# Sample-group state products of a hybrid decoder step: full-size SSD blocks, queue passes between tiny products, GLA sample queries built earlier

## The chip, the core and the metric

One core of a Trainium2 chip runs the whole step. TensorE multiplies into PSUM; VectorE (DVE), ScalarE (ACT) and GpSimd (POOL) work beside it; SyncE (SP) and POOL issue DMAs. The metric is the device time in microseconds (us) of one execution. Lower is better.

## The reference, cut to what matters

Two trunk layers work on 288 token columns: 256 prompt tokens and 32 sample tokens (8 sequences of 4). Each layer projects x with many weight matrices, runs three mixers (SSD, mLSTM, GLA), gates and merges them, and then runs a PEER expert stage. Each mixer carries a state; for the sample group each of the 8 sequences has its own state, which its 4 tokens read and then update. The read of the SSD state is the second term of `y`:

```
y = (jnp.einsum('btsgh,bsghp->btghp', w, xc)
     + jnp.einsum('btgn,bghpn->btghp', cc, h) * jnp.exp(lam)[..., None])
```

There are 2 groups g of 4 heads h, with 64 state rows n and 64 channels p. In GLA the read is `qc * exp(lam)` times S, with 4 heads of 64 by 128; in mLSTM it is C times q, with 4 heads of 128 by 128.

## The kernel before, in words

**The queue of passes.** Each layer's large projections are a list of jobs (`self.jobs`). A generator `feed` (L300) works them off: for each of 8 row blocks of one 128-column weight block it issues three passes of 288 columns (L325, L327, L329: high part by high, high by low, low by high), so a column block is 24 passes. Before a half block is multiplied, ACT (L210) rounds its weights to the high part and DVE (L211) subtracts to get the low part; these splits are issued three halves ahead. `pump(n)` issues the next n passes, and returns without any when the list is empty.

**The mixers.** `ssd`, `mlstm` and `gla` are generators. `mixers` (L392) steps each that is alive once per round, and after every step pumps `RATE` passes (18 with two alive, 6 with three, 14 with two once the SSD branch is queued). The order of instructions on every engine is therefore written out by hand: this loop fixes it. All three go over two prompt chunks of 128 tokens and then the sample segment of 32.

**The list of jobs.** 63 column blocks do not wait for the end of mLSTM or GLA: 51 from the start, then the 4 of the SSD branch and 8 gates, which `ssd` adds at its end. Only when mLSTM ends does `branch(1, ...)` add 4 blocks of its branch and 4 gates (to 71). GLA's end adds 4, and then 8 of the output projection (83).

**The SSD sample segment.** `ch` (L641) is the decayed query, with group g on partitions 64g to 64g+63. For each of 8 heads two sorts of products add into `py`: `w` by `xdt` (L656), and 8 products, one per sequence, of a 64x64 state `hS` with 4 columns of `ch` (L663). Two heads form a step, then the generator yields: 4 steps. L669 adds the skip term. `START` passes are pumped before the first chunk.

**mLSTM sample states.** 8 units (head, half of the sequences): 4 products of a 128x128 state with 4 columns (L895), one update product (L898), then a yield.

**GLA sample states.** `QS` (L1096) is the query with one head's rows kept, made by two DVE instructions at the start of the sample segment. L1104 adds the local part into `pos`, then 4 units of 4 products of a 128x128 state `SS` with 8 columns of `QS` (L1117). POOL makes masked values for the updates in `masked` (its instruction is L380) of mLSTM and GLA. `QE`, from which `QS` is made, is complete at L1043, after the last decay level.

**mLSTM's end.** After the last unit come the norm, a wait until the gates are projected (`until`, then `sigmoids` L486 and the GLA gate's sigmoids L949, each pumping 4 passes), a table load for exponentials (L358), the split of the branch (L957, L960, L962) and `branch(1)`. `merge` (L1210) normalises at the layer's end.

Of the kernel before, what the change touches and what calls it, by code (L numbers as in the profile page):

```python
# [7 lines left out]
F32 = mybir.dt.float32  # L8
# [8 lines left out]
OP = mybir.AluOpType  # L17
# [5 lines left out]
TP = 256  # L23
# [13 lines left out]
STEPS = 76  # L37
SIGM = 4
SIGS = 6
START = 24  # L40
NO = 2
NG = 8
NB = 16
# [23 lines left out]
def bc(ap, shape):  # L67
    return ap.to_broadcast(shape)


class Kernel:
# [483 lines left out]
    def ssd(self):  # L555
        ve, ac, gp, pe, L, I, O, mx = self.ve, self.ac, self.gp, self.pe, self.L, self.I, self.O, self.mx
        act4, act2, dt = self.xs, self.bcs, self.dt
# [21 lines left out]
        ys = act4  # L579
        self.pump(START)  # L580
        yield 1
        for sg, (c0, n) in enumerate(SEGS):
            cols = slice(c0, c0 + n)
            smp = sg == 2
            if sg == 1:
# [6 lines left out]
                hS = [self.st2(f"hS{i}", [128, 2, 4, 64], I["h"][L][:, 2 * i:2 * i + 2]) for i in range(4)]  # L592
# [12 lines left out]
            xdt = self.w2("xdt")  # L605
# [13 lines left out]
            r4 = lambda a: a[:, :4 * n].rearrange("p (h t) -> p h t", t=n)  # L619
            w = []  # L620
            for g in range(2):
                pd = r4(self.ps_rc("pd"))
                for h4 in range(4):
                    pe.matmul(pd[:n, h4], bc(self.ident[:8, g * 4 + h4:g * 4 + h4 + 1], [8, n]), lam[:, cols],
                              start=True, stop=True)
# [11 lines left out]
            if sg:  # L637
                el = r4(self.w2("el", n))
                ac.activation(el, pl, AF.Exp)
                ch = r4(self.w2("ch", n))  # L640
                ve.tensor_tensor(ch, el, bc(act2[:, None, 1, cols], [128, 4, n]), op=OP.mult)  # L641
            yield 1
            for g in range(2):
                pcb = self.ps_rc(f"pcb{g}")[:, :n]
                pe.matmul(pcb[:n], act2[g * 64:(g + 1) * 64, 0, cols], act2[g * 64:(g + 1) * 64, 1, cols],
                          start=True, stop=True)
                ve.tensor_tensor(w[g][:n], w[g][:n], bc(pcb[:n, None, :], [n, 4, n]), op=OP.mult)
            yield 1
            py = [self.ps_rc(f"py{g}")[:, :2 * n].rearrange("p (i t) -> p i t", t=n) for g in range(2)]
            for i in range(4):  # L650
                g = i // 2
                for h2 in range(2):
                    h = 2 * i + h2
                    h4 = h - 4 * g
                    po = py[g][64 * h2:64 * h2 + 64, i % 2]
                    pe.matmul(po, xdt[:n, h * 64:(h + 1) * 64], w[g][:n, h4], start=True, stop=(sg == 0),  # L656
                              skip_group_check=True)
                    if sg == 1:
                        pe.matmul(po, hP[g * 64:(g + 1) * 64, h4], ch[g * 64:(g + 1) * 64, h4],
                                  start=False, stop=True, skip_group_check=True)  # L660
                    elif sg == 2:
                        for b in range(8):
                            pe.matmul(po[:, 4 * b:4 * b + 4], hS[b // 2][g * 64:(g + 1) * 64, b % 2, h4],  # L663
                                      ch[g * 64:(g + 1) * 64, h4, 4 * b:4 * b + 4],
                                      start=False, stop=True, skip_group_check=True)
                if smp:
                    yield 1
            for i in range(4):
                ve.scalar_tensor_tensor(ys[i][:, cols], act4[i][:, cols], self.pc("sd", i), py[i // 2][:, i % 2],  # L669
                                        op0=OP.mult, op1=OP.add)  # L670
            yield 1

            if not smp:
# [10 lines left out]
            else:  # L684
                elb = el.rearrange("p h (b t) -> p b h t", t=4)
                for u in range(4):
                    ph = self.ps_rc("ph").rearrange("p (b h d) -> p b h d", h=4, d=64)
                    for b2 in range(2):
                        b = 2 * u + b2
# [28 lines left out]
        hi, lo = self.z4("bsh", F32R), []  # L718
# [8 lines left out]
    def mlstm(self):  # L727
        ve, ac, gp, pe, L, I, O, mx = self.ve, self.ac, self.gp, self.pe, self.L, self.I, self.O, self.mx
# [7 lines left out]
        b = self.row("b", 4)  # L736
# [47 lines left out]
        for sg, (c0, n) in enumerate(SEGS):  # L784
            cols = slice(c0, c0 + n)
            smp = sg == 2
            N4 = 4 * n
            r4 = lambda a: a[:, :N4].rearrange("p (h t) -> p h t", t=n)
# [90 lines left out]
            for h in range(4):  # L879
                pe.matmul(pn[:, h], vt[:n, h * 128:(h + 1) * 128], St[:n, h], start=(h == 0 or not smp), stop=(sg == 0),  # L880
                          skip_group_check=True)
# [4 lines left out]
            if smp:  # L886
                yield 1
                for u in range(8):
                    h, bh = divmod(u, 2)
                    if u + 2 < 8:  # L890
                        load(u + 2)
                    S = CS[u]
                    for b_ in range(4):
                        t0 = 16 * bh + 4 * b_
                        pe.matmul(pn[:, h, t0:t0 + 4], S[:, b_], qe[:, h, t0:t0 + 4], start=False, stop=True,  # L895
                                  skip_group_check=True)
                    pc_ = self.ps_rc("pc_").rearrange("p (b d) -> p b d", d=128)
                    pe.matmul(pc_, kst[:96, h * 128:(h + 1) * 128], vm[:96], start=True, stop=True)  # L898
                    if u < 7:
                        vm = mask(u + 1)  # L900
                    ve.tensor_tensor(S, S, bc(ec[:, h, 2 + 4 * bh:6 + 4 * bh].unsqueeze(2), [128, 4, 128]), op=OP.mult)
                    ve.tensor_tensor(S, S, pc_, op=OP.add)
                    gp.dma_start(O["sC"][L][:, h, 4 * bh:4 * bh + 4], S)
                    yield 1
# [8 lines left out]
            if not smp:  # L913
                pc_ = hd(self.ps_rc("pc_"))
                for h in range(4):
                    pe.matmul(pc_[:, h], kt[:n, h * 128:(h + 1) * 128], wv[:n, h * 128:(h + 1) * 128],
                              start=True, stop=True)
# [36 lines left out]
        hi, lo = self.z4("bmh", F32R, "mk"), self.z4("bml", F32R, "mv")  # L954
# [12 lines left out]
    def gla(self):  # L967
        ve, ac, gp, pe, L, I, O, mx = self.ve, self.ac, self.gp, self.pe, self.L, self.I, self.O, self.mx
# [54 lines left out]
        for l in range(7):  # L1023
            X, nt = nxt
            if l < 6:
                nxt = decayed(l + 1)
            else:

                QE = s2("QE")
                ac.activation(QE, lam, AF.Exp, scale=TAU)  # L1030
                ends = mx.tile([128, 2, 10], F32, tag="ends", name="ends")
                ve.tensor_copy(ends[:, :, 0:2], lam[:, :, 127:TP:128])
                ve.tensor_copy(ends[:, :, 2:], lam[:, :, TP + 3::4])
                KE = lam
                for c0, c1, n, e in ((0, TP, 128, ends[:, :, 0:2]), (TP, T, 4, ends[:, :, 2:])):
                    a = lambda x: x[:, :, c0:c1].rearrange("p h (n t) -> p h n t", t=n)
                    ve.tensor_tensor(a(KE), bc(e.unsqueeze(3), [128, 2, (c1 - c0) // n, n]), a(lam), op=OP.subtract)
                ac.activation(KE, KE, AF.Exp, scale=TAU)
                el = mx.tile([128, 2, 8], F32, tag="el", name="el")
                ve.tensor_copy(el, QE[:, :, TP + 3::4])  # L1040
                elc = mx.tile([128, 2], F32, tag="elc", name="elc")
                ve.tensor_copy(elc, QE[:, :, TP - 1])
                ve.tensor_tensor(QE, QE, q, op=OP.mult)  # L1043
                ve.tensor_tensor(KE, KE, k, op=OP.mult)
            yield 1
            for sg, (c0, n) in enumerate(SEGS):
                if c0 < nt:
                    pa = scores(X, X, sg)
                    for h2 in range(2):
                        ve.copy_predicated(att[sg][:n, h2::2], bc(self.masks[:n, None, l, :n], [n, 2, n]), pa[h2][:n])  # L1050
# [3 lines left out]
        for sg, (c0, n) in enumerate(SEGS):  # L1054
# [35 lines left out]
                vst = self.stack("vst", pv[:32], 512, False)  # L1090
            yield 1
            if smp:

                QS = self.w2("QS", n).rearrange("p (h g t) -> p h g t", g=2, t=32)
                for h2 in range(2):
                    ve.tensor_scalar(QS[:, :, h2], QE[:, :, cols], self.half[:, h2:h2 + 1], None, op0=OP.mult)  # L1096
                pos = self.ps_rc("pos")[:, :128].rearrange("p (h g t) -> p h g t", g=2, t=32)
                po2 = [pos[:, :, h2] for h2 in range(2)]
            else:
                po2 = [self.ps_rc(f"po{h2}")[:, :2 * n].rearrange("p (h t) -> p h t", t=n) for h2 in range(2)]  # L1100
# [7 lines left out]
            if smp:  # L1108
                for u in range(4):
                    hp, bh = divmod(u, 2)  # L1110
                    if u + 2 < 4:
                        load(u + 2)
                    S = SS[u]
                    vms = [mask(2 * hp + h2, bh) for h2 in range(2)]
                    for b in range(4):
                        t0 = 16 * bh + 4 * b
                        pe.matmul(pos[:, hp, :, t0:t0 + 4], S[:, b], QS[:, hp, :, t0:t0 + 4],  # L1117
                                  start=False, stop=True, skip_group_check=True)
                    ve.tensor_tensor(S, S, bc(el[:, hp, 4 * bh:4 * bh + 4].unsqueeze(2), [128, 4, 128]), op=OP.mult)
                    yield 1  # L1120
                    pst = self.ps_rc("pst").rearrange("p (b d) -> p b d", d=128)
                    for h2 in range(2):
                        pe.matmul(pst, kz[:96, hp, h2], vms[h2][:96], start=h2 == 0, stop=h2 == 1)
                    ve.tensor_tensor(S, S, pst, op=OP.add)
                    gp.dma_start(O["sS"][L][:, hp, 4 * bh:4 * bh + 4], S)
# [682 lines left out]
```

## Time and profile before

| | |
|---|---|
| device time, median of 3 runs | 2605.63 us (2599.55 to 2611.2) |
| profiled execution, device time | 2610.51 us |
| its span in the trace | 2608.7 us |
| mean granted TensorE clock | 0.965 of full |
| TensorE busy | 2507.6 us, 96% |
| VectorE busy | 2040.0 us, 78% |
| ScalarE busy | 1283.9 us, 49% |

The mixers run from the start to about 445 us for the first layer, and from about 1290 to 1740 us for the second. A TensorE that is shown busy can still be slow: the granted clock is told beside it, as a share of 2.4 GHz, and 0.5 is the lower of its two levels (1.2 GHz).

### The profile page before, as it was taken

How to read it: one execution, taken by the hardware profiler on the slowest of the kernel's cores; microseconds unless marked ns; L12 is line 12 of the kernel's file. 1: busy time of each engine (PE TensorE's matmuls, PEld its weight loads, DVE VectorE, ACT ScalarE, POOL GpSimd, SP SyncE). 2: the span in 40 equal slices, each digit the busy share in tenths (PEclk: the TensorE clock that was granted, in tenths of full speed). 3: DMA queues.
4: the chain of work that ended last, by engine and by line, in shares of the span. 5: the costliest groups of instructions: out<-in, count | busy, mean ns of one | idle time of the engine just before them, and what ended most of it. 6: DMA issues, size and time to landing. Idle time of an engine off the chain costs nothing. (4 is left out here: it accounts for less than half of the span.)

```text
span 2608.7 us, 45575 instructions
## 1 busy us (share of the span) xinstructions
PE 2507.6 (96%) x17206; PEld 2276.1 (87%) x17206; DVE 2040.0 (78%) x4018; ACT 1283.9 (49%) x2545; POOL 359.9 (14%) x362
## 2 busy tenths in 40 slices
PE   8999998999999999999989999989999999999998
PEld 8987897989999988888789878979999999788886
DVE  7647777699899958888685477775998999588885
ACT  6433555445554434444474344653455544444444
POOL 1000232150000012221020002222400000122210
PEclk9978999999999999999999798999999999999999
DMA  5422444446555568888545124435455455689884
GB/s 167 126 72 77 147 155 130 139 145 185 163 170 160 165 196 304 302 310 299 175 134 134 58 85 163 152 110 163 158 173 171 161 170 164 227 305 305 304 276 132
DMA packets 132029, 465.11 MB, mean 178 GB/s; under 512 B 15361, under 2 KB 17537, under 8 KB 131809
## 3 DMA queue, kind: packets, MB, share of 16 engines
q1 hardware_dynamic: 109728, 385.14, 45.3%
q0 software_dynamic: 22080, 77.06, 9.3%
q8 instruction: 135, 2.21, 0.3%
q14 instruction: 86, 0.70, 0.1%
HBM read 451.32 MB, written 10.82 MB: 177 GB/s over the span
## 5 line engine op out<-in xcount | busy, mean ns | idle before, releaser
L211 DVE TENSOR_TENSOR hl<-raw,hl 128x1024 fp32r<-128x1024 f32 (+1 forms) x832 | 874.9, 1056 | 313.4 <-ACT hl L210 298.1
L210 ACT ACTIVATE hl<-raw 128x1024 fp32r<-128x1024 f32 (+1 forms) x880 | 777.4, 887 | 493.6 <-PE pu L255 153.1
L1522 PE MATMUL acc<-hl,wh 128*128 128x512 f32 x2048 | 649.2, 397 | 9.2 <-ACT hl L210 8.0
L254 PE MATMUL pu<-hh,hl 128*128 128x256 f32 x2048 | 505.1, 287 | 12.8 <-ACT WA L1442 12.8
L255 PE MATMUL pu<-hl 128*128 128x256 f32 x2048 | 495.5, 281 | 0.0
L1522 PEld LDWEIGHTS acc<-hl,wh 128*128 128x128 f32 x2048 | 386.3, 189 | 106.3 <-ACT hl L210 10.7
L1522 PE MATMUL acc<-hl,wl 128*128 128x512 f32 x1024 | 408.0, 398 | 0.0
L254 PEld LDWEIGHTS pu<-hh,hl 128*128 128x128 f32 x2048 | 388.0, 189 | 15.0 <-ACT WA L1442 14.2
L255 PEld LDWEIGHTS pu<-hl 128*128 128x128 f32 x2048 | 388.2, 190 | 0.0
L327 PE MATMUL pz<-xl,hl 128*128 128x288 f32 x1008 | 329.0, 326 | 0.6 <-DVE xl L1630 0.3
L325 PE MATMUL pz<-xh,hl 128*128 128x288 f32 x1008 | 312.5, 310 | 13.5 <-ACT xh L210 6.5
L329 PE MATMUL pz<-xh,hl 128*128 128x288 f32 x1008 | 311.2, 309 | 1.2 <-DVE hl L211 1.0
L257 PE MATMUL pu<-hh,hl 128*128 128x256 f32 x2048 | 285.9, 283 | 2.4 <-DVE hl L211 2.2
L257 PEld LDWEIGHTS pu<-hh,hl 128*128 128x128 f32 x2048 | 261.2, 189 | 3.7 <-DVE hl L211 3.4
L1522 PEld LDWEIGHTS acc<-hl,wl 128*128 128x128 f32 x1024 | 193.4, 189 | 47.8
L210 ACT ACTIVATE wh<-WA 128x256 fp32r<-128x256 f32 x200 | 83.5, 417 | 278.0 <-PE acc L1522 275.8
L325 PEld LDWEIGHTS pz<-xh,hl 128*128 128x128 f32 x1008 | 201.6, 200 | 17.0 <-ACT xh L210 7.3
L327 PEld LDWEIGHTS pz<-xl,hl 128*128 128x128 f32 x1008 | 200.9, 199 | 17.6 <-issue 12.1
L329 PEld LDWEIGHTS pz<-xh,hl 128*128 128x128 f32 x1008 | 202.1, 200 | 7.1 <-issue 3.5
L1643 POOL DMA_INDIRECT gbuf<-in_u,se x64 | 61.7, 964 | 957.3 <-PE pu L257 705.3
L1482 DVE TENSOR_TENSOR oj<-dgd,dones 128x1024 int32<-128x1024 int32 x64 | 139.2, 2178 | 0.0
L211 DVE TENSOR_TENSOR wl<-WA,wh 128x256 fp32r<-128x256 f32 x200 | 84.5, 422 | 69.3 <-ACT wh L210 69.3
(582 smaller groups left out, 3515.6 us busy)
## 6 DMA issues: line engine op xcount, KB each, us to landing
raw<-in_ut SPq DMA_DIRECT2D x256, 512.0 KB, 3.8
raw<-in_v SPq DMA_DIRECT2D x256, 512.0 KB, 4.5
raw<-in_win SPq DMA_DIRECT2D x126, 512.0 KB, 3.6
raw<-in_wq SPq DMA_DIRECT2D x32, 512.0 KB, 3.6
raw<-in_wbr SPq DMA_DIRECT2D x24, 512.0 KB, 3.6
raw<-in_wout SPq DMA_DIRECT2D x16, 512.0 KB, 3.6
CS<-in_C SPq DMA_DIRECT2D x16, 256.0 KB, 4.0
out_sC<-CS POOLq DMA_DIRECT2D x16, 256.0 KB, 3.2
```

The lines of the kernel that those rows point to most:

```text
L210: self.ac.activation(hi, r, AF.Copy)
L211: (eng or self.ve).tensor_tensor(lo, r, hi.bitcast(F32), op=OP.subtract)
L254: self.pe.matmul(ps, wh[k], self.xh[:, k, :n], start=(k == 0), stop=False)
L255: self.pe.matmul(ps, wh[k], self.xl[:, k, :n], start=False, stop=False)
L257: self.pe.matmul(ps, wl[k], self.xh[:, k, :n], start=False, stop=(k == 7))
L325: self.pe.matmul(ps, hi[:, m], xh, start=(first and m == 0), stop=False)
L327: self.pe.matmul(ps, hi[:, m], xl, start=False, stop=False)
L329: self.pe.matmul(ps, lo[:, m], xh, start=False, stop=last)
L1482: ve.tensor_tensor(flat(oj).rearrange("p (q a b) -> p q a b", a=16, b=16), bc(words(gd.rearrange("p g k t -> p (g k) t")).unsqueeze(3), [1 ...
L1522: pe.matmul(acc[t][d], lhs[:, 128 * t:128 * t + 128], rhs, start=False, stop=last and n == 2, skip_group_check=True)
L1643: self.gp.indirect_dma_start(out=g, out_offset=None, in_=src, in_offset=bass.IndirectOffsetOnAxis(ap=ix[:, r:r + 1], axis=0))
```

## The change

For the sample segment of SSD the query goes into `chm`, a 256-column buffer in which the half that belongs to the other group is zero. Then one 128x128 block of two heads' states serves both groups: 2 products of 16 columns for each of 8 sequences, all adding into one PSUM tile, instead of 64 products of 4 columns. The `w` by `xdt` products come after them, all together, and L669 becomes 8 half-height instructions for this segment. After each sequence in SSD, and after every second state product of mLSTM and GLA, `pump(TINY)` issues 3 passes. `START` goes from 24 to 12. `QS` is made in GLA right after `QE`, into a buffer of its own.

```diff
-START = 24
+START = 12
+TINY = 3
...
-                ch = r4(self.w2("ch", n))
-                ve.tensor_tensor(ch, el, bc(act2[:, None, 1, cols], [128, 4, n]), op=OP.mult)
+                if smp:
+                    chm = self.w2("chm")[:, :256].rearrange("p (j g h t) -> p j g h t", j=2, g=2, h=2)
+                    for g in range(2):
+                        r = slice(64 * g, 64 * g + 64)
+                        ve.memset(chm[r, :, 1 - g], 0.0)
+                        ve.tensor_tensor(chm[r, :, g], el[r].rearrange("p (j h) t -> p j h t", h=2),
+                                         bc(act2[r, None, None, 1, cols], [64, 2, 2, n]), op=OP.mult)
...
+                pall = self.ps_rc("py")[:, :256].rearrange("p (j g h t) -> p j g h t", j=2, g=2, h=2)
+                for b in range(8):
+                    for j in range(2):
+                        a = lambda x: x[:, j, :, :, 4 * b:4 * b + 4].rearrange("p g h t -> p (g h) t")
+                        pe.matmul(a(pall), hS[b // 2][:, b % 2, 2 * j:2 * j + 2].rearrange("p h d -> p (h d)"), a(chm),
+                                  start=(b == 0 and j == 0), stop=False, skip_group_check=True)
+                    self.pump(TINY)
+                    if b % 2:
+                        yield 1
+                py = [[pall[:, j, g] for j in range(2)] for g in range(2)]
...
-                    elif sg == 2:
-                        for b in range(8):
-                            pe.matmul(po[:, 4 * b:4 * b + 4], hS[b // 2][g * 64:(g + 1) * 64, b % 2, h4],
-                                      ch[g * 64:(g + 1) * 64, h4, 4 * b:4 * b + 4],
-                                      start=False, stop=True, skip_group_check=True)
-                if smp:
-                    yield 1
...
@@ mlstm, sample units
                         pe.matmul(pn[:, h, t0:t0 + 4], S[:, b_], qe[:, h, t0:t0 + 4], start=False, stop=True,
                                   skip_group_check=True)
+                        if b_ % 2:
+                            self.pump(TINY)
...
@@ gla, after the last decay level
                 ve.tensor_tensor(QE, QE, q, op=OP.mult)
+                QS = mx.tile([128, 2, 2, 32], F32, tag="QS", name="QS")
+                for h2 in range(2):
+                    ve.tensor_scalar(QS[:, :, h2], QE[:, :, TP:], self.half[:, h2:h2 + 1], None, op0=OP.mult)
                 ve.tensor_tensor(KE, KE, k, op=OP.mult)
...
@@ gla, sample segment
-                QS = self.w2("QS", n).rearrange("p (h g t) -> p h g t", g=2, t=32)
-                for h2 in range(2):
-                    ve.tensor_scalar(QS[:, :, h2], QE[:, :, cols], self.half[:, h2:h2 + 1], None, op0=OP.mult)
...
@@ gla, sample units
                         pe.matmul(pos[:, hp, :, t0:t0 + 4], S[:, b], QS[:, hp, :, t0:t0 + 4],
                                   start=False, stop=True, skip_group_check=True)
+                        if b % 2:
+                            self.pump(TINY)
```

## Rows read from the trace of the kernel before

**Rows 1.** A stretch: length, busy time (x instructions) PE, PEld, DVE, ACT, POOL, granted clock, DMA.
```profile
147.90:188.60 40.70, 40.70 (x283) 35.03 (x283) 17.43 (x27) 13.24 (x26) 0.00 (x0) 0.71 0.16 51
```

**Rows 2.** Two stretches inside it, one after the other, same columns.
```profile
157.90:161.20 3.30, 3.30 (x43) 3.18 (x43) 3.12 (x6) 2.65 (x6) 0.00 (x0) 1.00 0.00 0
161.30:168.10 6.80, 6.80 (x28) 5.49 (x27) 1.38 (x3) 1.75 (x5) 0.00 (x0) 0.50 0.00 0
```

**Rows 3.** TensorE in order of time: start, us, instruction; one SSD step.
```profile
147.56 0.29 PE L329 MATMUL pz<-xh,hl 128*128 128x288 f32 x1
147.69 0.29 PE L325 MATMUL pz<-xh,hl 128*128 128x288 f32 x1
...
148.15 1.09 PE L663 MATMUL py<-ch,hS 64*64 64x4 f32 x16
...
150.65 0.30 PE L329 MATMUL pz<-xh,hl 128*128 128x288 f32 x1
...
151.06 0.44 PE L329 MATMUL pz<-xh,hl 128*128 128x288 f32 x1
151.30 0.44 PE L325 MATMUL pz<-xh,hl 128*128 128x288 f32 x1
```

**Rows 4.** The same view: local products in one run, a state unit, a return.
```profile
75.93 1.09 PE L656 MATMUL py<-w,xdt 128*64 128x128 f32 x16
...
282.98 0.95 PE L895 MATMUL pn<-qe,CS 128*128 128x4 f32 x8
283.79 0.48 PE L898 MATMUL pc__2962<-vm,kst 96*128 96x512 f32 x1
...
329.64 0.38 PE L325 MATMUL pz<-bsh,hl 128*128 128x288 f32 x1
329.86 0.30 PE L327 MATMUL pz<-bsl,hl 128*128 128x288 f32 x1
```

**Rows 5.** The same view, GLA's first sample unit [idle before <-releaser].
```profile
311.45 1.07 PE L1104 MATMUL pos<-att,vt 32*128 32x32 f32 x8
317.49 1.88 PE L1117 MATMUL pos<-QS,SS 128*128 128x8 f32 x8 [4.97 <-DVE QS L1096]
```

**Rows 6.** That moment on DVE, POOL and SP; landings of `SS`.
```profile
313.80 3.63 DVE L1096 TENSOR_SCALAR QS<-QE,half 128x64 f32<-128x64 f32 x2
...
314.18 3.03 POOL L380 TENSOR_TENSOR vm<-vst,bm 96x512 fp32r<-96x512 f32 x3
...
308.69 0.89 SPq L386 DMA_DIRECT2D SS<-in_S  x2
...
DMA to landing us min/median/max: 2.3/3.8/5.0
```

**Rows 7.** Stretch around that wait, columns of Rows 1.
```profile
311.40:328.60 17.20, 12.23 (x55) 11.93 (x55) 10.88 (x14) 1.89 (x3) 4.73 (x6) 0.60 0.52 177
```

**Rows 8.** L325 alone from the layer's start; columns: length, PE, PEld, clock, DMA.
```profile
0.00:349.40 349.40, 145.91 (x459) 95.41 (x459) 0.89 0.38 120
0.00:369.00 369.00, 159.35 (x504) 103.85 (x504) 0.90 0.39 123
```

**Rows 9.** TensorE in order of time: mLSTM's end, and the layer's normalisation.
```profile
349.36 0.38 PE L1143 MATMUL pr<-sq,ones 128*128 128x128 f32 x2
...
370.02 0.40 PE L325 MATMUL pz<-bmh,hl 128*128 128x288 f32 x1 [2.01 <-ACT hl L210]
...
452.39 0.85 PE L254 MATMUL pq<-hh,hl 128*128 128x288 f32 x2 [6.97 <-ACT hh L1256]
```

**Rows 10.** ScalarE in order of time at mLSTM's end.
```profile
355.68 1.28 ACT L486 ACT_TABLE_LOAD   x1
...
357.84 1.10 ACT L486 ACTIVATE gate<-gate 128x288 f32<-128x288 f32 x3
...
368.35 1.10 ACT L960 ACTIVATE bmh<-mq 128x288 fp32r<-128x288 f32 x3
```

**Rows 11.** Stretch after the normalisation's wait, columns of Rows 1.
```profile
452.40:458.30 5.90, 5.59 (x19) 4.46 (x19) 3.87 (x10) 5.73 (x11) 0.00 (x0) 0.51 0.00 0
```

More of the change, by code (lines that the diff above doesn't have):

```diff
@@ L639, in ssd @@
                 ac.activation(el, pl, AF.Exp)
-                ch = r4(self.w2("ch", n))
-                ve.tensor_tensor(ch, el, bc(act2[:, None, 1, cols], [128, 4, n]), op=OP.mult)
+                if smp:
[5 more added lines that the diff above has]
+                                         bc(act2[r, None, None, 1, cols], [64, 2, 2, n]), op=OP.mult)
+                else:
+                    ch = r4(self.w2("ch", n))
+                    ve.tensor_tensor(ch, el, bc(act2[:, None, 1, cols], [128, 4, n]), op=OP.mult)
             yield 1
@@ L648, in ssd @@
             yield 1
-            py = [self.ps_rc(f"py{g}")[:, :2 * n].rearrange("p (i t) -> p i t", t=n) for g in range(2)]
+            if smp:
+                pall = self.ps_rc("py")[:, :256].rearrange("p (j g h t) -> p j g h t", j=2, g=2, h=2)
[8 more added lines that the diff above has]
+                py = [[pall[:, j, g] for j in range(2)] for g in range(2)]
+            else:
+                py = [self.ps_rc(f"py{g}")[:, :2 * n].rearrange("p (i t) -> p i t", t=n) for g in range(2)]
             for i in range(4):
@@ L654, in ssd @@
                     h4 = h - 4 * g
-                    po = py[g][64 * h2:64 * h2 + 64, i % 2]
-                    pe.matmul(po, xdt[:n, h * 64:(h + 1) * 64], w[g][:n, h4], start=True, stop=(sg == 0),
+                    po = py[g][i % 2][64 * h2:64 * h2 + 64, h2] if smp else py[g][64 * h2:64 * h2 + 64, i % 2]
+                    pe.matmul(po, xdt[:n, h * 64:(h + 1) * 64], w[g][:n, h4], start=not smp, stop=(sg != 1),
                               skip_group_check=True)
@@ L660, in ssd @@
                                   start=False, stop=True, skip_group_check=True)
-                    elif sg == 2:
-                        for b in range(8):
-                            pe.matmul(po[:, 4 * b:4 * b + 4], hS[b // 2][g * 64:(g + 1) * 64, b % 2, h4],
-                                      ch[g * 64:(g + 1) * 64, h4, 4 * b:4 * b + 4],
-                                      start=False, stop=True, skip_group_check=True)
-                if smp:
-                    yield 1
             for i in range(4):
-                ve.scalar_tensor_tensor(ys[i][:, cols], act4[i][:, cols], self.pc("sd", i), py[i // 2][:, i % 2],
-                                        op0=OP.mult, op1=OP.add)
+                for lo, hi, p in ([(0, 64, py[i // 2][i % 2][:, 0]), (64, 128, py[i // 2][i % 2][:, 1])] if smp
+                                  else [(0, 128, py[i // 2][:, i % 2])]):
+                    ve.scalar_tensor_tensor(ys[i][lo:hi, cols], act4[i][lo:hi, cols], self.pc("sd", i, lo, hi), p[lo:hi],
+                                            op0=OP.mult, op1=OP.add)
             yield 1
```

## The prediction, made before the changed kernel was run

> **What bounds the kernel now.** I read the page's first part, and it says TensorE: busy for 96% of the span, as the table shows. A busy share says nothing about speed, so the second view is the one of stretches, with the granted clock. All that the change touches lies in the mixers of each layer, and there the reader should look for two kinds of loss. The first is work at the lower clock level: in the 40.7 us of the SSD sample steps TensorE never rests, but the mean clock is 0.71 [rows 1]. Inside it a step with its small products runs at full level, and the next 6.8 us run wholly at 0.50 [rows 2]; there are four steps per layer, and in each of the two layers each is followed by a fall. The second is waiting: the longest wait in the middle of the mixers is that for `QS`, 4.97 us [rows 5], and around it the clock is 0.60 [rows 7]. The second layer shows both again (0.71, 4.97 us). Third, I counted passes, since each inserted pass is only moved from later: L325 stands 459 times before L1143 and 504 times when the stream stops [rows 8], and 504 is 63 blocks of 8, exactly the list without mLSTM's branch. So the stream runs dry there already, with a wait of 2.01 us [rows 9].
>
> **The change part by part, for one layer.** From here on a pass costs 0.13 us at the upper level and 0.24 at the lower [rows 3], so of a stretch at the lower level 0.46 can be won back.
>
> *SSD products.* Between the last pass before a step and the second pass behind it lie 2.96 us [rows 3]; two passes of the stream in it take 0.26, so a step costs 2.7 and four cost 10.8. Each step holds 32 small passes (two runs of 16 as shown, each product being two passes). After the change there are 16 products, 32 passes, in eight groups of four. The nearest row for a 128x128 state with few columns is mLSTM's: eight passes from 282.98 to 283.79, 0.81 us, hence 0.41 for four [rows 4]. The return from such a group to the stream costs 0.22 - 0.13 = 0.09 [rows 4]. Eight groups: 4.0. The local products in one run: at most 1.09, the row of 16 with more columns [rows 4]. In all 5.1, so **-5.7**. The columns are 16, not 4; with the row of L1104 (32 columns, 1.07 for eight [rows 5]) it is -4.7, and if the returns are free -6.4. I take the L895 row, since its weights have the same size.
>
> *The clock behind these steps.* 40.7 us at 0.71 are 40.7 x 0.29 x 2 = 23.6 us at the lower level [rows 1]; 0.46 of that is 10.9. What comes ahead of each fall is over a microsecond of small products in one piece, twice per step; after the change no piece is longer than 0.41, and passes of the stream stand between. I expect the falls to go, and take **-10.0** because mLSTM's own products in the same rounds may still cause one. Bounds: 0 and -10.9. The time goes to the end only if nothing else is late: DVE is busy 17.4 and ACT 13.2 of the 40.7 us [rows 1], so both would still fit in the 25 us or so that remain.
>
> *`QS` early.* TensorE is ready after L1104, at about 312.5 [rows 5]. What is late next is the state itself: SP issues the load at 308.69 and it lands after 3.8 us in the median and 5.0 at most [rows 6], 312.5 to 313.7. A wait of 0 to 1.2 stays; I take 1.0, hence -4.0. The clock: 17.2 us at 0.60 are 13.8 at the lower level [rows 7], which end with the stretch, so they begin near 314.8, and 11.1 of them are work after the wait: up to -5.1. I take -4.5, together **-8.5** (bounds 0 and -10.1). The two instructions cost DVE under 0.5 us at their new place, on no wait of TensorE.
>
> The rows say why the old place was bad: the two `QS` instructions took 3.63 us together, while POOL made three masks from 314.18 to 317.21 [rows 6]. The Trainium skill, "SBUF — State Buffer", section "Who interferes with whom", says that a GpSimd instruction and a DVE instruction of this kind, or one with two SBUF inputs, shut each other out for a whole instruction. The trace agrees on `QS` (317.21 is where it gets through). By that rule the wait isn't removed but passed on to L1119, which has two such inputs and is next in DVE's queue, with the splits behind it; that is the third rival below.
>
> *Passes put between.* They are work that is only moved. New returns to the stream: two per mLSTM unit and one per GLA unit, 20 x 0.09 = 1.8. I take **+1.2**, between 0 and 1.8.
>
> *The moved passes are missing later.* Ahead of L1143 come 8 x 3 passes in SSD, 16 x 3 in mLSTM and 8 x 3 in GLA, less the 12 that `START` gives up: 84 passes, 28 of L325, 11.2 us. So at L1143 the count is 487 instead of 459, and 17 rows, 51 passes, 6.8 us, are left as cover for mLSTM's end instead of 135 passes. In the kernel before, the restart comes 370.02 - 349.36 = 20.7 us behind L1143 [rows 9]. Its chain is on ACT: from the first table load at 355.68 to the restart 14.3 us [rows 9, 10]. The load waited for gates that the stream was still making; these would now be ready, so it can come some 2.4 us behind L1143 (an estimate, between 0.4, which is L1143, and 6.3 as now). The chain itself gets shorter by the splits and copies of the passes that are gone and longer by about three sigmoids of 0.37 [rows 10]: I estimate 11.4, between 10 and 14.3. Restart 13.8 us behind L1143, with 11.2 us of work done earlier: 13.8 + 11.2 - 20.7 = +4.3 against now. TensorE then stands still for 13.8 - 0.4 - 6.8 = 6.6 us instead of 2.0. A wait of 6.97 us [rows 9] was followed by 5.9 us at the lower level [rows 11], so 0.46 x 5.9 = 2.7 more. Together **+7.0**, between +1 (10.4 us to the restart) and +16 (chain as long as now, 11.2, and 11.1 us at the lower level as behind the `QS` wait).
>
> *`START`* and the DVE instructions added (two fills, one more product, four more of L669) lie beside TensorE; SP gets the same loads. I cost them at nothing: if SSD's first rows aren't ready TensorE waits at its transposes for at most the 12 passes' 1.6 us, which I keep for the range. No new buffer is waited for that I can find: PSUM gets one tile less in these rounds, and `chm` is given back before the local products.
>
> Sum: -5.7 - 10.0 - 8.5 + 1.2 + 7.0 = -16.0 per layer, -32.0 for both. The profiled execution took 2610.5 us, so 2578.5; the median of the runs is 4.9 lower (0.2%), which gives 2573.6, rounded to **2574**. Its own range, with the terms' inner bounds, is 2561 to 2587.
>
> **The rivals.** First, *the cover is enough*: the ACT chain shrinks to its shortest and the dry stream costs +1. For it: ACT is only half busy. Against: two table loads and some sixteen sigmoids can't be passed over. -22 per layer, 2562. Second, *the dry stream costs in full*, +16: the chain isn't shortened. -7 per layer, 2592. Third, *DVE's block is passed on* to L1119 and the splits behind it come up to 3.0 us late [rows 6]: -13 per layer, 2580; against it, splits are made three halves ahead, 36 passes or 4.7 us. Fourth, *the change doesn't do what it says* for the clock: TensorE falls behind each SSD step as before, because L880, L916 and L920 stand in the same rounds. Without the -10.0: -6 per layer, 2594. Fifth, and slower: *the pieces pull the clock down elsewhere*. From 282.98 to 311.45 [rows 4, 5] mLSTM's units run at the upper level (0.81 for eight passes against 1.88 in GLA's first unit at the lower). If cutting them into pieces of four, with changes of form between, made this whole stretch run at the lower level, it would cost 28.5 x 0.85 = 24 us per layer; net +8, or 2622. It decides from 16.0 / 0.85 = 19 us of it. Against: more passes of the stream stand among the same products than before.
>
> **How the numbers follow.** Forecast 0.55, cover enough 0.12, dry in full 0.10, block passed on 0.10, clock unchanged 0.08, clock down elsewhere 0.05. Some 0.5% (13 us) is what a measurement of this kernel can tell from no change, so faster means below 2592.6. The forecast, the cover and the passed block lie there, 0.77, with about a third of the two that end at the edge, 0.06: 0.83. Same 0.12, slower 0.05. The range reaches from 2554 (cover enough, and the inner bounds) to 2594, which leaves out the slower case and the outer parts of the second and fourth.
>
> **What would show it.** Right: the four SSD steps at a clock near 1, and the stretch of rows 1 some 15 us shorter in work; GLA's first L1117 with a wait near 1 us, ended by the load and not by DVE; about 487 rows of L325 before L1143; and a wait of 5 to 8 us at L325's first pass on `bmh`, ended by ACT, with a fall of the clock behind it. Wrong: a wait there of 2 us or of over 10, a clock of 0.7 in the SSD steps, a new wait for DVE near L1117, or waits for DVE between the SSD steps because the rounds have become shorter than the chains beside them.

## The result and the profile after

The changed kernel takes 2575.11 us (median of 4 runs, 2571.87 to 2582.07) beside 2608.04 us: a ratio of 0.9873, 95% interval [0.9846, 0.99]. The forecast was 2574. The profiled execution took 2582.07 us, its span is 2580.3; it is the slowest of the four, with a mean granted clock of 0.970 where the others have 0.978 to 0.979 (0.965 in the profiled execution before). Of gla_passes, an experiment below, one run of six (2666.72 us, with a granted clock of 0.855) is left out of its median.

The page's first lines after (busy time and share of the span, instructions). TensorE lost 31 us of busy time, DVE and ACT did the same work as before:

```profile
PE 2477.0 (96%) x17014; PEld 2253.5 (87%) x17014; DVE 2036.9 (79%) x4032; ACT 1285.4 (50%) x2545; POOL 363.1 (14%) x362
```

To see where the time went I cut each layer's mixers at the same instructions in both kernels, and took 0.1315 us for every stream pass from each stretch, so that passes that were only moved drop out. What is left, in us, for both layers of one trace of before and of two traces of after (the second trace is an experiment below), and the means per layer:

| stretch, without its stream passes | before | after | after, second trace | change of the mean |
|---|---|---|---|---|
| first pass to first SSD state product | 41.8, 32.2 | 39.7, 37.8 | 36.6, 33.0 | -0.2 |
| SSD steps, to their last product | 27.0, 27.1 | 14.0, 14.0 | 14.0, 14.0 | -13.1 |
| to the first mLSTM state product | 56.8, 54.1 | 52.4, 54.0 | 50.1, 50.4 | -3.8 |
| mLSTM units, to GLA's local sample product | 17.4, 17.4 | 23.3, 21.8 | 20.2, 20.2 | +4.0 |
| to GLA's second sample unit | 13.7, 13.3 | 3.6, 3.6 | 3.6, 5.5 | -9.4 |
| to mLSTM's end (L1143, now L1165) | 5.9, 5.9 | 5.9, 5.9 | 5.9, 5.9 | 0.0 |
| to the restart behind it | 2.4, 2.4 | 6.6, 6.6 | 6.6, 6.6 | +4.2 |
| to the expert stage | 19.4, 19.4 | 21.1, 21.1 | 20.8, 21.4 | +1.7 |

The sum is -16.6 per layer; the prediction's was -16.0.

**SSD steps.** The stretches of the two layers' steps after (length, busy time and instructions of each engine, granted clock, DMA share, GB/s):

```profile
144.30:171.00 26.70, 26.68 (x213) 23.54 (x211) 18.35 (x29) 14.73 (x30) 0.00 (x0) 1.00 0.25 80
1427.80:1454.50 26.70, 26.67 (x213) 23.53 (x211) 18.40 (x29) 14.69 (x30) 0.00 (x0) 1.00 0.24 80
```

The clock is 1.00, where [rows 1] had 0.71: all four falls of each layer are gone. A group of four passes, in TensorE's timeline, and its return to the stream:

```profile
144.35 0.52 PE L665 MATMUL py<-chm,hS 128*128 128x16 f32 x4
144.71 0.38 PE L328 MATMUL pz<-xl,hl 128*128 128x288 f32 x1
144.93 0.29 PE L330 MATMUL pz<-xh,hl 128*128 128x288 f32 x1
```

**GLA's first unit**, timeline of TensorE: the wait of [rows 5] is gone, and no rest of it is left in this layer.

```profile
304.03 1.07 PE L1124 MATMUL pos<-att,vt 32*128 32x32 f32 x8
305.03 0.61 PE L1137 MATMUL pos<-QS,SS 128*128 128x8 f32 x4
```

**What is late now.** TensorE's longest waits in the first layer (line, what it waited for, total, times, longest):

```profile
PE pz L326 <- ACT hl L211: 7.4, 2, 6.4
...
PE pz L326 <- ACT sr L481: 1.8, 2, 1.6
...
PE pz L326 <- DVE mixed L506: 1.4, 1, 1.4
```

The longest of the first line (6.4) stands at mLSTM's end, where it was 2.0 [rows 9]. The other two stand inside the mLSTM units: that for `sr` was 0.3 before, that for `mixed` is new. The chain at mLSTM's end, on ACT, from the first table load to the split of the branch, and TensorE's restart:

```profile
339.02 1.28 ACT L487 ACT_TABLE_LOAD   x1
...
346.52 1.28 ACT L359 ACT_TABLE_LOAD   x1
347.81 1.11 ACT L980 ACTIVATE bmh<-mq 128x288 fp32r<-128x288 f32 x3
```

```profile
350.43 0.61 PE L326 MATMUL pz<-bmh,hl 128*128 128x288 f32 x1 [6.36 <-ACT hl L211]
```

L1165 stands at 336.73, so the load comes 2.3 us behind it, the restart 13.7; 487 rows of L326 lie before it.

### The profile page after: what moved, and what is told of

Its sections match the earlier page's. It is cut to its first block, busy times and chain, and to the rows that moved or that the text cites. A ratio compares the mean times of both kernels' runs of the same rounds, so it can differ in the third digit from the quotient of the medians.

```text
span 2580.3 us, 45205 instructions
## 1 busy us (share of the span) xinstructions
PE 2477.0 (96%) x17014; PEld 2253.5 (87%) x17014; DVE 2036.9 (79%) x4032; ACT 1285.4 (50%) x2545; POOL 363.1 (14%) x362
## 5 line engine op out<-in xcount | busy, mean ns | idle before, releaser
L326 PE MATMUL pz<-xh,hl 128*128 128x288 f32 x1008 | 312.8, 310 | 11.1 <-ACT xh L211 6.1
L326 PEld LDWEIGHTS pz<-xh,hl 128*128 128x128 f32 x1008 | 202.2, 201 | 13.3 <-ACT xh L211 6.2
```

The lines of the kernel that those rows point to most:

```text
L326: self.pe.matmul(ps, hi[:, m], xh, start=(first and m == 0), stop=False)
```

## The experiments

Theory at the start, the prediction's: the clock fell in SSD because tiny products stood in one piece, and passes between them keep it up (C). Rival: what counts is the products, not what stands between (D). All experiments have `QS` early.

**Four kernels that cross the two.** p128_passes is the changed kernel without the passes in mLSTM and GLA:

```diff
-                        if b_ % 2:
-                            self.pump(TINY)
```

(and in GLA the same two lines, with `b` for `b_`).

> The changed kernel with the three passes put in only after each sequence of SSD; the passes put into the mLSTM and GLA units are taken out again (72 passes per layer). In the trace of the changed kernel the stretch from the first mLSTM state product to L1124 holds, beside its stream passes at 0.13 us, 23.3 us (first layer) and 21.7 us (second), against 17.4 us before: new waits of 1.6 us (for ACT at 266.13) and 1.4 us (for DVE at 297.39) and a fall of the clock. And the wait at mLSTM's end is 6.4 us against 2.0, with a fall behind it. Theory A (the passes inside the units cause both): both go back to what they were, the cover at L1165 is about 126 passes instead of 54, the wait there 2 to 3 us: some 10 us per layer less, 2555 us. Rival B (both come from SSD having become shorter, so that the chains of ACT and DVE beside it are late whatever the units hold): 0 to 4 us per layer less, 2567 to 2575 us.

p128_none also takes out those in SSD:

```diff
                                   start=(b == 0 and j == 0), stop=False, skip_group_check=True)
-                    self.pump(TINY)
```

> As p128_passes, but with no pass put between the 128x128 products of SSD either: four products stand in one piece, four pieces, with the loop's own passes between the pieces. Theory C (passes of the stream between the tiny products keep the clock up): TensorE falls to 1.2 GHz behind the SSD steps again, which costs up to 10 us per layer, 2575 us, and the granted clock of the SSD stretch is 0.7 to 0.8. Rival D (products of full size are enough, since there are half as many and they are over sooner): the SSD stretch stays at 1.00, and the time is that of p128_passes within 4 us (2551 to 2559 us).

p64_passes has the old products with 24 passes between them:

```diff
                                       start=False, stop=True, skip_group_check=True)
+                            if b == 3:
+                                self.pump(2)
+                        self.pump(1)
```

> SSD's products as in the kernel before (64x64, four columns), but cut into pieces of four with one or two passes of the stream between, 24 passes in all as in the changed kernel; QS early, START 12, nothing put into the mLSTM and GLA units. Theory C: the SSD stretch is at full clock, and what is left against p128_passes is only the 5.7 us per layer of the products themselves and some 0.7 us of returns to the stream: 13 us more, 2568 us. Rival D (the size of the products): the falls stay, 10 us more per layer, 2588 us.

p64_none is the kernel before with `QS` built behind `QE` and

```diff
-START = 24
+START = 12
```

> The kernel before with only two of the changes: QS made early, and START 12. SSD as before. If the parts add up as worked out, GLA's first sample unit saves the 10 us per layer that the trace of the changed kernel shows (wait 4.97 to 0 and 13.6 us less at the lower level), the falls behind the four SSD steps stay, and the time is some 2588 us. If the time saved at GLA is only given back at mLSTM's end, where the next wait is (2.0 us before), the wait there grows to 6 us or more and the time is 2598 us or more.

Measured, ratio to before in brackets: p128_passes 2567.33 [0.9794, 0.9842], p128_none 2567.16 [0.979, 0.984], p64_passes 2607.11 [0.9963, 0.9998], p64_none 2596.98 us [0.9932, 0.9977]. The first layer's SSD steps, columns as above; p128_none:

```profile
143.60:167.30 23.70, 23.46 (x189) 20.32 (x187) 17.09 (x27) 13.15 (x27) 0.00 (x0) 1.00 0.20 68
```

p64_passes:

```profile
140.70:180.50 39.80, 39.80 (x279) 32.78 (x277) 16.62 (x25) 12.27 (x25) 0.00 (x0) 0.79 0.15 43
```

p64_none:

```profile
140.40:174.50 34.10, 34.10 (x255) 28.50 (x254) 15.97 (x24) 11.12 (x22) 0.00 (x0) 0.74 0.16 47
```

C falls, D holds. Without a pass between them the large products keep the clock at 1.00, and the stretch without its stream passes is 14.2 us as against 14.0. With passes between them the small ones still lose it. TensorE's timeline of p64_passes shows how short its pieces are:

```profile
153.62 0.62 PE L663 MATMUL py<-ch,hS 64*64 64x4 f32 x8
154.17 0.40 PE L327 MATMUL pz<-xl,hl 128*128 128x288 f32 x1
154.41 0.29 PE L329 MATMUL pz<-xh,hl 128*128 128x288 f32 x1
154.63 0.62 PE L663 MATMUL py<-ch,hS 64*64 64x4 f32 x8
```

0.55 us from one to the next form, a quarter of the 2.2 us that a step had in one go, and yet 17.1 us of the stretch run at the lower level (17.6 before). The kernel is even slower than p64_none. Two limits: its pieces are longer than the changed kernel's (0.36 us), with one or two passes between them and not three; three between small products were not run. And D's own time for it, 2588, is 19 us too low: 12 of these come from p128_passes, which the sum took at 2555, and the other 7 stay open.

p128_passes also answers for the passes in the units. Its waits in the first layer:

```profile
PE pz L326 <- ACT hl L211: 3.1, 2, 2.0
```

The wait at mLSTM's end is back at 2.0, the waits for `sr` (1.6) and `mixed` (1.4) are gone, and the mLSTM stretch holds 17.6 us: theory A by its mechanism. Of its 10 us per layer the traces show 8 (4 in the units, 4 at the end), but 3.2 come back in GLA's first unit, where this kernel has a fall of 6.8 us in both layers (7.3 and 7.2 us for that row of the table). So 2567, not 2555. What brings that fall is not shown: no wait of over 0.3 us stands there.

p64_none separates the parts. `QS` with START gives 0.45% (12 us; 20 expected). Its wait at mLSTM's end stays at 2.0, so it isn't given back there; the row of GLA's first unit falls to 4.7 and 7.6 (in the second layer `SS` is waited for, 0.8, and a fall follows), but the units behind it take 7.7 and 6.4 instead of 5.9, since TensorE now comes to a pass before DVE has mixed (0.3 twice in the first layer, once in the second, and 0.8 ahead of them in the first). From there to p128_none, the SSD products, it is 30 us by the medians, 37 by the ratios; 31 were forecast.

**Beside the changed kernel itself.** after_again is the changed kernel once more; none_s24 is p128_none with

```diff
-START = 12
+START = 24
```

and gla_passes is p128_none with `if b % 2: self.pump(TINY)` in the GLA units alone.

> The changed kernel itself, unaltered, for a second trace and beside the others of this call. In its first trace the first layer's mixers had become 17.9 us shorter and the second layer's only 7.0, the difference lying ahead of the SSD steps: there 5.4 us stood at the lower level in the kernel before and 19.8 in the changed one, in a part of the program that the change touches only by START. Theory E (which of the falls ahead of the SSD steps come differs from execution to execution): the stretch from the first pass to the first state product of the second layer again has another share at the lower level, anywhere between 3 and 20 us, and the falls inside the mLSTM units and behind mLSTM's end, which follow waits, come again at the same places. Rival F (START 12 causes the added falls): 19 to 20 us at the lower level in the second layer again. Time 2575 us under both.

> p128_none (128x128 products, QS early, no pass put in anywhere) with START back at 24. Theory E (START only moves 12 passes): the time of p128_none within 4 us, 2563 to 2571 us. Rival F (START 12 costs falls in the stretch ahead of SSD, or on the contrary hides something there): 5 us or more away from it on either side.

> p128_none with the passes put into the GLA units alone. In p128_none the last two GLA units and what follows to L1165 hold 5.2 us beside the stream, in the changed kernel 3.4, and the cover at mLSTM's end falls from 150 to 126 passes, at which p128_passes still waited only 2.0 us. Theory I: 2 us less per layer than p128_none, 2563 us. Rival J: the passes in the GLA units cost waits as those in the mLSTM units did, 2570 us or more.

Measured: after_again 2569.79 [0.9834, 0.9892], none_s24 2572.42 [0.9826, 0.9876], gla_passes 2565.51 us [0.9811, 0.9865]. The second layer from its first pass to the SSD steps; before:

```profile
1313.00:1445.40 132.40, 129.98 (x957) 122.20 (x957) 89.37 (x200) 73.82 (x167) 14.56 (x23) 0.98 0.47 135
```

after:

```profile
1291.40:1427.80 136.40, 134.26 (x942) 126.71 (x943) 89.06 (x201) 72.86 (x166) 14.57 (x23) 0.93 0.45 130
```

after_again:

```profile
1285.90:1417.50 131.60, 129.43 (x942) 121.99 (x943) 89.09 (x201) 72.57 (x166) 14.59 (x23) 0.97 0.46 135
```

The same kernel, 0.93 once and 0.97 once: the first trace's meagre second layer was chance (E). The fall inside an mLSTM unit that the first trace showed (6.8 and 3.4 us, in the row of the mLSTM units 3.1 and 1.6) is missing in the second, so it too was chance; the three waits, 6.4, 1.6 and 1.4, come again to the tenth. none_s24 lies 5.3 us above p128_none and 3.4 above its repetition, with intervals that overlap: what START does to the whole time is not settled. One thing in its trace is plain:

```profile
PE pos L1133 <- DMA SS<-in_S: 0.9, 1, 0.9
```

That is the rest of the `SS` wait that the prediction expected. With START 24 the load is issued 2.8 us ahead of GLA's local product, as before (308.69 to 311.45), in p128_none, which differs by START alone, 4.3 (287.24 to 291.52), in the changed kernel 4.7 (299.35 to 304.03). START does not settle it: with the same 4.3 us p128_none waits in neither layer, but p64_none, t128_twice, t128_four, rows64 and cols64 wait 0.8 to 1.3 us in their second. gla_passes shows neither gain nor loss.

**Which property of the products.** t128_twice, t128_four, rows64 and cols64 are p128_none with the state products cut up. The edit of cols64, its main lines (rows64 has `hS` and `chm` on the 64 rows of one group and both heads' columns, and a PSUM tile for each group; t128_twice and t128_four all rows and columns, 8 and 4 columns of `chm`):

```diff
...
-                        pe.matmul(a(pall), hS[b // 2][:, b % 2, 2 * j:2 * j + 2].rearrange("p h d -> p (h d)"), a(chm),
...
+                                pe.matmul(pall[o, j, g, h, 4 * b:4 * b + 4], hS[b // 2][:, b % 2, 2 * j + h],
+                                          chm[:, j, g, h, 4 * b:4 * b + 4],
...
```

> p128_none with each 128x128 product cut into two of 8 columns, one for each group, so that 64 products, 128 small passes, stand in the SSD segment as in the kernel before, but each uses all 128 rows and columns of weights. By the row of mLSTM (0.41 us for four passes) they take 13 us per layer instead of 6.5. Theory G (the falls come from products that use a quarter of the array, 64 rows by 64 columns): the SSD stretch stays at 1.00 and the time is that of p128_none plus 13 us, 2580 us. Rival H (the falls come from the number of small products or the time they take, whatever their size): the falls come back, 10 us more per layer, 2600 us.

> p128_none with each 128x128 product cut into four of 4 columns: 64 products, 128 small passes in the SSD segment, as many and with as many columns as in the kernel before, but each with full weights. (t128_twice holds 32 products and 64 passes, not the 64 and 128 that its expectation says.) t128_twice added 3.1 us per layer for 16 products; 48 products add 9.3: 2586 us. Theory G (the quarter of the array that a product uses makes the falls): SSD stretch at 1.00, 2586 us. Rival H (the number of small products makes them): mean clock there 0.7 to 0.8, some 10 us per layer more, 2606 us.

> As t128_four, 64 products of 4 columns, but each with 64 rows and 128 columns of weights (one group's state rows, two heads), one PSUM tile per group. By the row of L663 of the kernel before a pass starts 0.06 us after the last, so 128 passes take some 8 us against 3.2 in p128_none: 5 us per layer, 2577 us, with the clock up. Theory G1 (the rows that are left empty make the falls): the clock of the SSD stretch falls as before (0.74), 10 us per layer more, 2597 us. Theory G2 (the empty columns do): 1.00 here. Rival H: falls here and in both others of this call.

> As t128_four, 64 products of 4 columns, but each with 128 rows and 64 columns of weights (both groups' rows, one head). Loading half the columns should pace a pass like L663's, 0.06 us: 2577 us with the clock up. Theory G1 (empty rows): 1.00 here, 2577 us. Theory G2 (empty columns): the clock falls, 2597 us. If neither this nor rows64 falls, it takes both halves empty, as in the 64x64 products.

> p128_none unaltered, beside the three others of this call, which differ from it in the state products alone. 2567 us; SSD stretch at 1.00; the falls elsewhere vary, so that the second trace tells how much of a difference between two traces is chance: SSD's own stretch 23.6 us again within 0.1.

Measured: t128_twice 2574.87 [0.9844, 0.9895], t128_four 2612.99 [0.9983, 1.0031], rows64 2597.27 [0.9945, 0.9974], cols64 2576.07 [0.9855, 0.992], none_again 2569.0 us [0.9833, 0.9884]. For each kernel one line of TensorE's timeline, the first step's state products (start, length), and one of the stretch of the four steps, with the columns as above. p128_none, whose stretch is shown above (none_again has 23.6 us there again, in both layers, at 1.00):

```profile
143.63 0.96 PE L664 MATMUL py<-chm,hS 128*128 128x16 f32 x8
```

cols64:

```profile
138.25 1.41 PE L667 MATMUL py<-chm,hS 128*64 128x4 f32 x32
```

```profile
138.20:164.00 25.80, 25.80 (x284) 22.31 (x283) 17.23 (x27) 13.29 (x27) 0.00 (x0) 1.00 0.22 62
```

t128_twice:

```profile
141.03 1.85 PE L665 MATMUL py<-chm,hS 128*128 128x8 f32 x16
```

```profile
141.00:167.80 26.80, 26.80 (x221) 23.92 (x219) 17.18 (x27) 13.37 (x27) 0.00 (x0) 1.00 0.19 60
```

rows64:

```profile
138.21 2.47 PE L667 MATMUL py<-chm,hS 64*128 64x4 f32 x32
```

```profile
138.20:173.10 34.90, 34.90 (x284) 30.41 (x283) 17.99 (x28) 13.37 (x27) 0.00 (x0) 0.85 0.16 46
```

t128_four:

```profile
141.71 3.91 PE L667 MATMUL py<-chm,hS 128*128 128x4 f32 x32
```

```profile
141.70:186.90 45.20, 45.20 (x285) 40.77 (x283) 17.69 (x28) 13.44 (x27) 0.00 (x0) 0.74 0.13 36
```

The number of products isn't it: cols64 has as many as before (128 passes of 4 columns) and stays at 1.00. A full array isn't enough: t128_four has it and falls, to 23.9 us at the lower level. What all the runs have in common is how long TensorE spends on small products in a step: 0.96, 1.41 and 1.85 us were followed by no fall. Behind 2.2 (before, two runs of 1.09), 2.2 to 2.5 in pieces (p64_passes) and 3.6 or more (t128_four) the clock fell, and behind 2.47 (rows64) it fell in five of eight steps. Half-empty rows fit nearly as well: every kernel with 64-row weights fell, and only t128_four fell without them; and rows64, with more time in its products than before, has less of its stretch at the lower level (10.2 us against 17.6; its trace is of the fastest of its ten runs, 2583.64 us, so others may have more). The two can't be told apart by these runs, and I leave it open which one decides. G1 named both times (2597 and 2577), and that rows64 would fall and cols64 would not. Its time for rows64 is met in part by luck, since the clock there is 0.85 and 0.90 in the two layers, not 0.74. And G fell on t128_four, which should have stood at 1.00; H as a matter of the number fell on cols64, and as a matter of time it leaves rows64's smaller share unexplained. (t128_twice holds 32 products; its expectation counts 64.)

## Why the prediction was right, and where it was not

The time and the sum were right and one reason was wrong. That the sum fits so closely is partly luck: the passes put between cost 2.8 us more per layer than priced, and the other terms together came out 3.4 lower.

*SSD products and their clock* (-5.7 and -10.0). Of the 13.1 us less in the steps' stretch, 0.46 of the 17.6 us at the lower level are 8.1 and the rest, 5.0, the products. That is 0.7 less than forecast, although the new products were overpriced: 0.36 us for four passes instead of 0.41, and 0.58 for the local ones (170.56 to 171.14) instead of 1.09. Where the 0.7 went is open; the split hangs on the 0.46. The fall behind the last step reached 6.3 us into the next stretch (181.75 to 188.6 before), another 2.9 us, which makes 11.0 for the clock, the upper bound. The sizes were right. The reason, no piece longer than 0.41 us and passes between, was not: p128_none has pieces of 0.96 us, no passes between and no fall; p64_passes has passes between pieces of 0.55 and falls. The 24 passes put in for it bought nothing.

*`QS`* (-8.5): -9.4. Instead of 1.0 no wait was left in three of the four layers traced, and 0.27 in the fourth. I had costed START at nothing, but it shifts the stream against the issue of the `SS` load: with START 24 (none_s24) the wait is 0.9 in both layers. It is not START alone, as the waits with START 12 above show. Third rival: the masks do hold up DVE's next instructions. In the timelines of DVE and POOL after:

```profile
306.57 1.51 DVE L212 TENSOR_TENSOR hl<-raw,hl 128x512 fp32r<-128x512 f32 x1 [0.21 <-ACT hl L211]
308.01 1.52 DVE L1141 TENSOR_TENSOR SS<-SS,el 128x512 f32<-128x512 f32 x1
```

```profile
305.48 3.50 POOL L381 TENSOR_TENSOR vm<-vst,bm 96x512 fp32r<-96x512 f32 x3
```

Beside the masks a split takes 1.51 us, where one at 304.87 takes 0.68; L1141 takes 1.52, and in the kernel before (L1119, at 319.40) 0.69. The Trainium skill, "SBUF — State Buffer", "Who interferes with whom", says that a DVE instruction with two SBUF inputs contends with a GpSimd instruction that reads SBUF. The trace agrees: 0.8 us each. TensorE waited for neither, as splits are made ahead; the rival's 3.0 us did not reach it.

*Passes put between* (+1.2): +4.0, the term that was furthest off, since I had priced only the returns to the stream. More passes in a unit also bring TensorE sooner to a pass whose PSUM place ACT or DVE has yet to empty: 1.6 us behind ACT's table load (264.04, 1.28 us), 1.4 us behind what DVE does for GLA's norm, both gone in p128_passes. The remaining 1.2 on the mean are falls of the first trace. In the second trace, without these falls, the stretch is 2.8 longer than before, which the two waits cover: the 16 returns to the stream in it, priced at 0.09 each, don't show.

*Missing passes at the end* (+7.0): +5.9. The steps were nearly exact: count 487 (487), load 2.3 us behind L1165 (2.4), chain from the load to the restart 11.4 us (11.4), wait 6.4 (6.6). The stretch behind it is 1.7 longer, where a fall of 2.7 was forecast. But 1.2 of that stand in p128_none too, with a fall of 3.4 us behind its wait of 2.01, so the longer wait itself brought about 0.5. That the stream "runs dry there already" is true of the list (504 rows), but the wait was misread as missing cover: with 125, 137 and 149 passes of cover (p128_passes, before, p128_none) it is 2.01 us each time, since the restart then comes 19.0, 20.6 and 22.2 us behind L1165 and moves with the last pass. Between 53 and 125 passes lies the point where cover begins to be short: 13.7 us of chain less the 2.0 and the 0.4 to the first pass are 86 passes (an estimate).

*Ahead of SSD* (0): -0.2 on the mean, but single layers differ: by 4.8 us between the two traces of the changed kernel (37.8 and 33.0), by 10 us among all kernels' first layers (33.6 in rows64, 43.6 in none_s24). Behind SSD, winning clock back has another limit: where only 6.8 us instead of 30.2 ran at the lower level (after_again, first layer), TensorE stood 8.6 us instead of 5.1, most of it behind DVE's chain of mLSTM. In the waits of that trace (before, `hr` cost 1.7, `col` 2.0 and `St` nothing):

```profile
PE pa L1016 <- DVE hr L926: 2.6, 1, 2.6
...
PE pa L1016 <- DVE col L824: 1.7, 1, 1.7
...
PE pa L1016 <- DVE St L851: 1.0, 1, 1.0
PE pa L1016 <- DVE St L872: 1.0, 1, 1.0
```

The first rival failed on the wait of 6.4, the second on the chain (11.4, not 14.3), the fourth on the clock; the fifth's fall came in one unit of each layer of the first trace (6.8 and 3.4 us) and not in the second, far from its 19 us.

So the gain is that of two parts: `QS` early with START, 12 us (6 to 18 by its interval), and the products, 30 us. The passes put in gave nothing in SSD and took some in mLSTM. Without them p128_none runs 2567.16 and 2569.0 us against 2575.11 and 2569.79. The traces give it about 6 us per layer (3.8 in the mLSTM units, 4.7 behind L1165, less 2.3 in GLA), but the intervals of the two repetitions overlap ([0.9833, 0.9884] for none_again, [0.9834, 0.9892] for after_again), so that it is not shown to be faster.

## What to carry to other kernels

When small products are followed by a fall of TensorE's clock although it never idles, make their time shorter, with weights that fill the array's rows (which of the two counts is open); one or two passes of other work between pieces of them did not help here. A filler pass isn't free where it stands: it costs whatever it makes TensorE reach too soon, and the cover that it takes from a later chain. Count that cover against the chain's own length, not against the wait seen before, and take a second trace before explaining a difference of five microseconds in one stretch.

## What the hardware showed that I had not expected

With the same 4 columns and the same number of passes (128 in the four steps), a pass with 128 rows and 64 columns of weights starts 42 ns behind the last one (cols64: 1.34 us from the first of 32 to what follows), one with 64 by 64 some 64 ns (before: 1.02 for 16), with 64 by 128 75 ns (rows64: 2.40 for 32), and with 128 by 128 109 ns (t128_four: 3.49 for 32 at 177.77; its step shown above ran in part at the lower level), all at the upper level. Half the rows were faster with 128 columns and slower with 64; the runs do not show why.
